# A rotary embedding kernel writes 512 KB of zeros to its output first, from the ScalarE queue

## Chip, cores, metric

One core of a Trainium2 chip. The metric is the time of one execution in device microseconds.

## The reference

```python
batch, seq_len, num_heads, head_dim = 8, 2048, 16, 64     # x: (8, 2048, 16, 64) float32; cos, sin: (2048, 32)
x1, x2 = x[..., :32], x[..., 32:]
out1 = x1 * cos - x2 * sin                                # cos, sin broadcast over batch and heads
out2 = x1 * sin + x2 * cos
out  = concatenate([out1, out2], axis=-1)                 # float32
```

x and the output are 67.1 MB each, 8.4 MB per batch.

## The kernel before

```python
P = 128; J = S // P          # 16 rows of the sequence on each partition
NBUF = 5
const_pool = ...tile_pool(bufs=1)
io_pool  = ...tile_pool(bufs=NBUF)        # five float16 tiles of one batch each
tmp_pool = ...tile_pool(bufs=1)           # one float16 tile v

head = const_pool.tile([P, JA, H, D], f32)                 # JA = 2
nc.sync.dma_start(out=head..., in_=x0[:, 0:JA, :]...)      # 1 MB, the first rows of batch 0
# --- the change goes in here ---
nc.sync.dma_start(out=sin_f, in_=sin...)                   # 256 KB
nc.sync.dma_start(out=cos_f, in_=cos...)                   # 256 KB

def load(b):                                               # float32 in DRAM -> float16 in SBUF
    xt = io_pool.tile([P, J, H, D], f16)
    nc.gpsimd.dma_start(out=xt..., in_=x[b]...)
    return xt

def store(b, xt):                                          # float16 in SBUF -> float32 in DRAM
    nc.gpsimd.dma_start(out=out[b]..., in_=xt)

def rotate(xt):                                            # 26.2 us on VectorE
    v = tmp_pool.tile([P, J, H, D], f16)
    nc.vector.tensor_mul(out=v[:, :, :, 0:Dh], in0=xt[:, :, :, Dh:D], in1=neg_b)
    nc.vector.tensor_mul(out=v[:, :, :, Dh:D], in0=xt[:, :, :, 0:Dh], in1=sin_b)
    nc.vector.tensor_mul(out=xw, in0=xw, in1=cos_b)
    nc.vector.tensor_add(out=xa, in0=xa, in1=v...)

tiles = [load(b) for b in range(NBUF)]
nc.scalar.copy(...)                                        # head rows, sin, -sin, cos to float16
for b in range(B):
    rotate(tiles[b])
    if b < B - 1: store(b, tiles[b])
    if b + NBUF < B: tiles.append(load(b + NBUF))
# ... the last batch is stored in three parts
```

All bulk transfers but the first and the last rows (1 MB each, from SyncE) are issued from GpSimd and so share one queue, in program order. Loads 5, 6 and 7 reuse the tiles of batches 0, 1 and 2 and wait for those stores.

## Time and profile before

| | before |
|---|---|
| time, median of 3 runs | 317.48 us |
| span of the profile | 315.6 us |
| DMA share, 2.5 to 313 us, in three long stretches | 1.00 or more |
| VectorE busy | 209.2 us (66%) |
| VectorE ends its last rotation | 263.7 us |

The page of the kernel before: busy time of the engines, the busy tenths in 40 slices, and the queues.

```profile
DVE 209.2 (66%) x32; ACT 6.8 (2%) x6; POOL 9.4 (3%) x21
DVE  0009599999999999999979999990009994000000
DMA  9899999999999999999999999999999999999998
q0 software_dynamic: 2448, 99.09, 98.0%
q1 hardware_dynamic: 576, 2.62, 2.2%
HBM read 67.63 MB, written 67.11 MB: 427 GB/s over the span
```

Here q0 is the queue of GpSimd and q1 that of SyncE. VectorE has idle slices at the start, before its last rotation and during the last 51 us. The DMA row has none. The windows of the same kernel give the DMA share in the column before the last; it is a little over 1 because the recorded times of neighbouring packets overlap: a row of a store is recorded at 2.45 us, but on an engine the rows follow each other every 2.41 us.

```profile
2.50:100.00 97.50, 72.33 (x12) 3.66 (x4) 2.62 (x5) 1.00 1.02 224
100.00:200.00 100.00, 98.07 (x16) 0.00 (x0) 3.01 (x6) 1.00 1.00 346
200.00:313.00 113.00, 38.75 (x6) 1.90 (x1) 2.27 (x5) 1.00 1.01 395
```

The timeline of the kernel before: start, duration, engine, line, operation, and in brackets the idle time before it and what ended that.

```profile
5.45 1.90 ACT L75 CAST xt<-head 128x2048 f16<-128x2048 f32 x1 [3.43 <-DMA head<-in_x_dram]
23.51 4.43 DVE L67 TENSOR_TENSOR v<-xt,neg_h 128x8192 f16<-128x8192 f16 x1 [23.51 <-DMA xt<-in_x_dram]
35.55 0.62 ACT L81 CAST cos_h<-cos_f 128x512 f16<-128x512 f32 x1 [17.98 <-DMA cos_f<-in_cos_dram]
54.18 0.54 POOL L58 DMA_DIRECT2D out_dram<-xt  x1 [50.14 <-DVE xt L72]
121.83 0.53 POOL L51 DMA_DIRECT2D xt<-in_x_dram  x1 [41.14 <-DMA out_dram<-xt]
237.47 4.42 DVE L67 TENSOR_TENSOR v<-xt,neg_h 128x8192 f16<-128x8192 f16 x1 [24.82 <-DMA xt<-in_x_dram]
```

Read it so: rotation 0 starts when load 0 has landed; cos lands late and holds it up once more. Store 0 is issued at 54 us but has landed only at 121.8 us, when load 5 is let go: it stood behind five loads. Rotation 7 (last line) waits 24.8 us for its load. So VectorE waits for the DMA engines at both ends, and they never wait for VectorE.

### The profile page before, as it was taken

The numbers are of one execution on the slowest core, as the hardware profiler recorded it, in microseconds if no ns is written. First come the engines' busy times: TensorE is split into PE (matmuls) and PEld (weight loads), VectorE is DVE, ScalarE is ACT, GpSimd is POOL, SyncE is SP. The second block draws the span as 40 slices with busy tenths as digits, with TensorE's granted clock in tenths as the row PEclk, the third lists the DMA queues.
The fourth block names the chain that finished last, engine by engine and source line by source line (L and its number), as shares of the span: only waits on it lengthen the run. The fifth ranks groups of instructions, "written<-read, shape, count | busy, mean of one in ns | idle before, by whom it ended". The sixth has DMA issues, their size and how long they took to land.

```text
span 315.6 us, 126 instructions
## 1 busy us (share of the span) xinstructions
DVE 209.2 (66%) x32; ACT 6.8 (2%) x6; POOL 9.4 (3%) x21
## 2 busy tenths in 40 slices
DVE  0009599999999999999979999990009994000000
ACT  4010000000000000000000000000000002000000
POOL 3000000000000000010000000100000001000000
DMA  9899999999999999999999999999999999999998
GB/s 278 184 261 207 200 249 216 199 199 249 216 199 266 399 424 507 399 332 233 233 199 199 390 407 399 399 532 266 199 224 507 399 399 498 432 399 399 432 424 341
DMA packets 3024, 101.71 MB, mean 322 GB/s; under 512 B 336, under 2 KB 336, under 8 KB 592
## 3 DMA queue, kind: packets, MB, share of 16 engines
q0 software_dynamic: 2448, 99.09, 98.0%
q1 hardware_dynamic: 576, 2.62, 2.2%
HBM read 67.63 MB, written 67.11 MB: 427 GB/s over the span
## 4 chain that ended last, share of the span: by engine, by line
issue 25%; DMA 23%; DVE 21%; another core or an unknown queue 13%; POOL 1%; ACT 1%; SPq 0%; POOLq 0%; DVEq 0%; ACTq 0%
DMA xt<-in_x_dram 12%; DMA cos_f<-in_cos_dram 11%; DVE xt L70 8%; DVE xt L72 8%; DVE v L68 3%; DVE v L67 1%; ACT head L105 1%; POOL out_dram L58 1%; POOL xt L51 0%; ACT cos_h L81 0%; SPq L45 0%; SPq L36 0%; POOLq L58 0%; DVEq L67 0%
## 5 line engine op out<-in xcount | busy, mean ns | idle before, releaser
L70 DVE TENSOR_TENSOR xt<-xt,cos_h 128x16384 f16<-128x16384 f16 x8 | 69.5, 8692 | 4.2 <-ACT cos_h L81 3.9
L72 DVE TENSOR_TENSOR xt<-xt,v 128x16384 f16<-128x16384 f16 x8 | 69.5, 8692 | 0.3
L67 DVE TENSOR_TENSOR v<-xt,neg_h 128x8192 f16<-128x8192 f16 x8 | 35.4, 4425 | 50.1 <-DMA xt<-in_x_dram 49.9
L68 DVE TENSOR_TENSOR v<-xt,sin_h 128x8192 f16<-128x8192 f16 x8 | 35.3, 4417 | 0.0
L51 POOL DMA_DIRECT2D xt<-in_x_dram x8 | 4.4, 560 | 117.1 <-DMA out_dram<-xt 116.3
L105 ACT CAST head<-xt 128x2048 f32<-128x2048 f16 x1 | 1.9, 1897 | 227.6 <-DVE xt L72 227.6
L58 POOL DMA_DIRECT2D out_dram<-xt x7 | 3.7, 535 | 87.8 <-DVE xt L72 87.8
L95 POOL DMA_DIRECT2D out_dram<-xt x1 | 0.5, 531 | 50.5 <-DVE xt L72 50.5
L75 ACT CAST xt<-head 128x2048 f16<-128x2048 f32 x1 | 1.9, 1898 | 3.4 <-DMA head<-in_x_dram 3.4
L75 ACT ACT_TABLE_LOAD x1 | 1.3, 1283 | 0.7 <-PEq L127 0.7
L81 ACT CAST cos_h<-cos_f 128x512 f16<-128x512 f32 x1 | 0.6, 617 | 18.0 <-DMA cos_f<-in_cos_dram 18.0
L79 ACT CAST sin_h<-sin_f 128x512 f16<-128x512 f32 x1 | 0.6, 617 | 9.1 <-DMA sin_f<-in_sin_dram 9.1
L80 ACT ACTIVATE neg_h<-sin_f 128x512 f16<-128x512 f32 x1 | 0.6, 624 | 0.0
L97 POOL DMA_DIRECT2D out_dram<-xt x1 | 0.5, 531 | 0.0
L127 POOL MEMSET const-float32-0.0<- 128x1 f32 x1 | 0.1, 98 | 0.2 <-issue 0.2
L127 POOL MEMSET const-bfloat16-1.0<- 128x1 bf16 x1 | 0.1, 101 | 0.0
L127 POOL MEMSET const-float32-1.0<- 128x1 f32 x1 | 0.1, 98 | 0.0
L127 POOL MEMSET const-uint8-127<- 128x1 uint8 x1 | 0.1, 98 | 0.0
## 6 DMA issues: line engine op xcount, KB each, us to landing
xt<-in_x_dram POOLq DMA_DIRECT2D x7, 4096.0 KB, 41.1
out_dram<-xt POOLq DMA_DIRECT2D x1, 4608.0 KB, 42.3
xt<-in_x_dram POOLq DMA_DIRECT2D x1, 3584.0 KB, 22.2
out_dram<-xt POOLq DMA_DIRECT2D x1, 2560.0 KB, 47.9
head<-in_x_dram SPq DMA_DIRECT2D x1, 1024.0 KB, 4.7
out_dram<-head SPq DMA_DIRECT2D x1, 1024.0 KB, 8.4
sin_f<-in_sin_dram SPq DMA_DIRECT2D x1, 256.0 KB, 15.2
cos_f<-in_cos_dram SPq DMA_DIRECT2D x1, 256.0 KB, 33.9
```

The source lines that it names most:

```text
L51: nc.gpsimd.dma_start(out=xt[:, j0:J, :, :].rearrange("p j h d -> p (j h d)"), in_=x[b].rearrange("(p j) h d -> p j (h d)", j=J)[:, j0:J, ...
L58: nc.gpsimd.dma_start(out=out[b].rearrange("(p j) h d -> p (j h d)", j=J), in_=xt)
L67: nc.vector.tensor_mul(out=v[:, :, :, 0:Dh], in0=xt[:, :, :, Dh:D], in1=neg_b)
L68: nc.vector.tensor_mul(out=v[:, :, :, Dh:D], in0=xt[:, :, :, 0:Dh], in1=sin_b)
L70: nc.vector.tensor_mul(out=xw, in0=xw, in1=cos_b)
L72: nc.vector.tensor_add(out=xa, in0=xa, in1=v.rearrange("p j h d -> p (j h d)"))
L75: nc.scalar.copy(out=tiles[0][:, 0:JA, :, :].rearrange("p j h d -> p (j h d)"), in_=head.rearrange("p j h d -> p (j h d)"),)
L79: nc.scalar.copy(out=sin_h, in_=sin_f)
L80: nc.scalar.mul(out=neg_h, in_=sin_f, mul=-1.0)
L81: nc.scalar.copy(out=cos_h, in_=cos_f)
L95: gate = nc.gpsimd.dma_start(out=dst, in_=src)
L105: nc.scalar.copy(out=head.rearrange("p j h d -> p (j h d)"), in_=src)
```

## The change

The intent: 512 KB of zeros go to the first contiguous 512 KB of the output early on, from the ScalarE queue, and are overwritten by the result. The zeros use the buffer of v (same tag, one buffer), as v has less than 1 KB per partition left beside it.

```diff
+    W = 1024
+    zero = tmp_pool.tile([P, W], f32, tag="v")
+    nc.vector.memset(zero, 0.0)
+    nc.scalar.dma_start(
+        out=out[0].rearrange("s h d -> (s h d)")[0 : P * W].rearrange("(p f) -> p f", p=P),
+        in_=zero,
     )
```

The order of the instructions on each engine is otherwise unchanged. Two waits are new: the first multiply of rotation 0 and store 0 both wait for the zeros.

More of the change, by code (lines that the diff above doesn't have):

```diff
@@ L38 @@
         in_=x0[:, 0:JA, :].rearrange("p j f -> p (j f)"),
+    )
+    W = 1024
[4 more added lines that the diff above has]
+        in_=zero,
     )
```

## The prediction

> **What bounds the kernel now.** The 16 DMA engines, from start to end. Read by window, the DMA share is 0.93 or more from 2.5 to 314 us of the 315.6 us span; VectorE is busy 66%, ScalarE 2% (the page). The packet records agree: a row of a full batch takes 2.45 us (stores) or 2.43 us (loads) on an engine, 26.8 GB/s, 428 GB/s for 16; the float32 side of all transfers is 134.7 MB, and 134.7 MB / 428 GB/s = 314 us. Loads and stores simply add up.
>
> By the timeline VectorE ends rotation 7 at 263.7 us, and 51 us of stores follow. The first store is issued at 54 us, but the loads ahead of it on its queue keep the engines busy until about 101 us: 45 us of slack.
>
> **What the change adds.**
> - A memset of 128x1024 float32 on VectorE, about 1 us (estimate from the Trainium skill, "VectorE: DVE Perf Modes", section on zero memsets: one cycle per element), while VectorE idles until 23.5 us. Cost 0.
> - One DMA issue on ScalarE (0.4 us, as on SyncE); ScalarE waits for the head rows until 5.45 us anyway. Cost 0.
> - 512 KB more for the DMA engines: 8 packets of 4 KB on each. Packets of 2 KB took 96 ns and of 8 KB 309 ns, so about 167 ns each (interpolated): **1.34 us per engine**. The engines have no gap, so it is added to the end. Another issuing queue gives no more bandwidth (Trainium skill, "DMA: Bandwidth & Descriptors", section "Issuing engines are not separate DMA queues"); the trace agrees in that the queues' shares add up to 100%.
> - New waits: the first multiply of rotation 0 waits until the zeros have landed (they share the buffer of v), and so does store 0 (same bytes of the output). I expect them to land 5 to 20 us in, so neither wait is the last: the multiply waits for load 0 (23.5 us, now about 25), store 0 for VectorE (54 us).
>
> **What it moves.** A 2 KB packet of the tables gets one turn per 2.1 to 2.4 us packet of the loads. Before, some of them slip in before load 0 starts; the zeros now take that time. So cos lands 4 to 9 us later, the multiplication by cos (36.2 us) starts at 40 to 45 us, and rotations 0 to 4 shift as much. VectorE waits for loads at 158.6 us (1.6 us) and before rotation 7 (24.8 us), where the shift vanishes. Every store has tens of us of work ahead of it in the queue, so the order of transfers stays. On the critical path: only the 1.34 us.
>
> **Predicted time.** 317.48 + 1.34 = 318.8 us; 8 in 10: 317.9 to 320.2. Faster by over 2%: 1%; within 2%: 97%; slower by over 2%: 2%.
>
> **What would show it.** 128 more packets, of 4 KB, near 0.17 us each; written bytes up from 67.11 to 67.63 MB; DMA share still full; each landing of a bulk transfer about 1.3 us later (rotation 7 starts at 238.8 instead of 237.5 us); cos later by more than that.
>
> **What would make it wrong.** If the zeros land late (after 30 us), rotation 0 waits for them; still hidden unless it costs over 40 us. If small packets disturb bulk ones (slower 64 KB packets), the cost is larger. If the engines have idle time at the start that the zeros fill, it is smaller, down to 0.5 us. A fixed cost of a third queue would show outside the DMA-busy stretch.

## The result, and the profile after

318.70 us, median of 4 runs (318.46 to 319.15), against 317.42 us for the kernel before (4 runs). The ratio is 1.0041, 95% interval 1.0026 to 1.0056, which is +1.3 us (0.8 to 1.8). The ratios are not quite the ratios of the medians, nor of the plain means of the listed times (big_zeros below: 1.0309 against 1.0314). A difference in us below is this ratio less 1, times the median of the kernel before in the same rounds.

The page of the changed kernel: engines, slices, queues, and the new memset among the groups.

```profile
DVE 210.1 (66%) x33; ACT 6.8 (2%) x6; POOL 9.4 (3%) x21
DVE  1008899999999999999969999990008994000000
DMA  9999999999999999999999999999999999999998
q10 hardware_dynamic: 144, 0.52, 0.4%
HBM read 67.63 MB, written 67.63 MB: 427 GB/s over the span
L42 DVE MEMSET zero<- 128x1024 f32 x1 | 0.9, 912 | 1.0 <-PEq L134 1.0
```

A third queue has appeared (q10, that of ScalarE) with 0.52 MB, the written bytes are up by the same, and the rate over the span is still 427 GB/s. The windows of the changed kernel over the same stretches are again full:

```profile
2.50:100.00 97.50, 73.09 (x12) 4.82 (x5) 2.62 (x5) 1.00 1.04 229
100.00:200.00 100.00, 95.96 (x16) 0.00 (x0) 2.12 (x4) 1.00 1.00 346
200.00:313.00 113.00, 40.10 (x6) 1.90 (x1) 3.16 (x6) 1.00 1.00 390
```

The timeline of the changed kernel, the same instructions as before with the issue of the zeros in front (lines of the file moved by 7):

```profile
1.97 0.37 ACTq L43 DMA_DIRECT2D out_dram<-zero  x1
5.53 1.90 ACT L82 CAST xt<-head 128x2048 f16<-128x2048 f32 x1 [1.88 <-DMA head<-in_x_dram]
25.22 4.42 DVE L74 TENSOR_TENSOR v<-xt,neg_h 128x8192 f16<-128x8192 f16 x1 [23.29 <-DMA out_dram<-zero]
34.79 0.62 ACT L88 CAST cos_h<-cos_f 128x512 f16<-128x512 f32 x1 [18.48 <-DMA cos_f<-in_cos_dram]
53.42 0.54 POOL L65 DMA_DIRECT2D out_dram<-xt  x1 [49.38 <-DVE xt L79]
123.18 0.54 POOL L58 DMA_DIRECT2D xt<-in_x_dram  x1 [43.24 <-DMA out_dram<-xt]
238.82 4.42 DVE L74 TENSOR_TENSOR v<-xt,neg_h 128x8192 f16<-128x8192 f16 x1 [24.82 <-DMA xt<-in_x_dram]
```

Load 5 is let go 1.35 us later (123.18 against 121.83) and rotation 7 starts 1.35 us later (238.82 against 237.47). VectorE, on the other hand, is *early* in between: store 0 was ready 0.8 us sooner than before, and yet it landed later. That alone says that the transfers ahead of store 0, not VectorE, set the time.

Two things are not as predicted: rotation 0 was released by the zeros, and cos came earlier, not later. The DMA issues of the changed kernel (size and time from issue to landing):

```profile
xt<-in_x_dram POOLq DMA_DIRECT2D x1, 3584.0 KB, 23.5
out_dram<-zero ACTq DMA_DIRECT2D x1, 512.0 KB, 23.1
cos_f<-in_cos_dram SPq DMA_DIRECT2D x1, 256.0 KB, 33.1
```

The first of these, load 0, was issued at 1.25 us and so landed at 24.75 us; the zeros were issued at 1.97 us and landed at 25.07 us, 0.3 us behind. The packet records show why they took 23 us. Starts are counted from the first DMA packet of the execution; each figure in brackets is the number of packets in a group, over 16 engines.

```
load 0's first packet                3.4 us (each then takes 2.13 us on its engine)
zeros, 4 KB packets of 0.160 us      5.7 (16), 8.0 (16), 10.3 (16), 12.7 (16), 15.0 (16), 17.4 (16), 19.8 (16), 22.1 (16)
sin and cos, 2 KB packets            2.9 (101), then 10 to 16 per turn, 30 at 22.0, last at 30.0
```

The records do not name the engine, but groups of 16, one turn apart, say that each engine serves its queues in turn: one row of load 0 (2.13 us), one packet of zeros, one of the tables. The zeros came too late to run before load 0 began and so needed eight full turns. The same records show the cost directly: the rows of load 0 follow each other every 2.19 us in the kernel before and every 2.35 us in the changed one, 0.16 us for each of the eight packets of zeros, together 1.3 us.

### The profile page after: what moved, and what is told of

Its sections match the earlier page's. It is cut to its first block, busy times and chain, and to the rows that moved or that the text cites. A ratio compares the mean times of both kernels' runs of the same rounds, so it can differ in the third digit from the quotient of the medians.

```text
span 317.0 us, 131 instructions
## 1 busy us (share of the span) xinstructions
DVE 210.1 (66%) x33; ACT 6.8 (2%) x6; POOL 9.4 (3%) x21
## 4 chain that ended last, share of the span: by engine, by line
issue 25%; DMA 23%; DVE 21%; another core or an unknown queue 14%; POOL 1%; ACT 1%; SPq 0%; POOLq 0%; DVEq 0%; ACTq 0%
DMA xt<-in_x_dram 12%; DMA cos_f<-in_cos_dram 10%; DVE xt L77 8%; DVE xt L79 8%; DVE v L75 3%; DVE v L74 1%; ACT head L112 1%; POOL out_dram L65 0%; POOL xt L58 0%; ACT cos_h L88 0%; SPq L52 0%; SPq L36 0%; POOLq L65 0%; DVEq L74 0%
## 5 line engine op out<-in xcount | busy, mean ns | idle before, releaser
L75 DVE TENSOR_TENSOR v<-xt,sin_h 128x8192 f16<-128x8192 f16 x8 | 35.3, 4418 | 0.0
L42 DVE MEMSET zero<- 128x1024 f32 x1 | 0.9, 912 | 1.0 <-PEq L134 1.0
## 6 DMA issues: line engine op xcount, KB each, us to landing
xt<-in_x_dram POOLq DMA_DIRECT2D x1, 3584.0 KB, 23.5
```

The source lines that it names most:

```text
L42: nc.vector.memset(zero, 0.0)
```

## The experiments

Main theory ("bytes"): the engines are full from 2.5 us to the last 2 us, so the cost is the engine time of the added packets, 128 packets x 160.4 ns / 16 engines = 1.28 us, wherever they run. Rivals: the later start of rotation 0 (25.2 instead of 23.5 us), the VectorE work, or a fixed cost of a DMA on a third queue. Twelve runs were made, all with a correct result: nine other kernels, the changed kernel once more, and the kernel before twice.

| run | difference, us (95%) | first multiply, us | rotation 7, us |
|---|---|---|---|
| after_again | +1.2 (0.8 to 1.6) | 25.7 | 238.6 |
| memset_only | 0.0 (-0.3 to 0.4) | 24.4 | 238.2 |
| zeros_on_sync | +1.0 (0.6 to 1.3) | 51.8 | 238.8 |
| other_buffer | +1.4 (1.0 to 1.7) | 25.1 | 238.6 |
| tiny_zeros | -0.3 (-0.7 to 0.0) | 24.0 | 237.1 |
| big_zeros | +9.8 (9.4 to 10.3) | 47.6 | 248.0 |
| cos_on_scalar | -0.2 (-0.5 to 0.2) | 27.6 | 237.5 |
| copy_in_dram | +1.5 (1.0 to 2.0) | 25.3 | 238.5 |
| tiny_late | -0.1 (-0.5 to 0.3) | 24.6 | 237.7 |
| behind_loads | +36.1 (35.5 to 36.6) | 103.5 | 287.3 |

### after_again: the changed kernel once more

> The changed kernel again, to pin its cost within a tighter interval and to see what of its trace repeats. Every theory: the kernel before plus 1.3 us (1.1 to 1.5). Turn theory (one packet of the zeros per bulk packet of load 0 on each engine): the zeros land about 25 us into the span again, in 8 groups of 16 packets. Landing of cos: I could not predict it; if it differs by up to one bulk packet (2.4 us) from the 34.8 us of the first profile, the earlier landing there was chance and not an effect of the change.

Edit: none. 318.84 us, ratio 1.0037 (1.0025 to 1.0049). The zeros ran in the same eight groups of 16, from 5.7 to 22.2 us, and released rotation 0 again. The copy of cos started at 32.2 us, 2.55 us earlier than in the first profile of the same kernel (a little more than the 2.4 us written down): that landing moves by about one turn from run to run.

### memset_only: without the DMA

```diff
-    nc.scalar.dma_start(
-        out=out[0].rearrange("s h d -> (s h d)")[0 : P * W].rearrange("(p f) -> p f", p=P),
-        in_=zero,
-    )
```

> The memset without its DMA. Byte theory (the engines are full, 128 packets of 160 ns cost 1.28 us per engine): 0 us beside the kernel before (within 0.2). Rival that says the VectorE work or the new tile in the buffer of v costs: up to +1.3 us. The first multiply starts at about 23.5 us, released by load 0.

317.75 us, ratio 1.0001 (0.9989 to 1.0013). The memset and its tile show no cost (within -0.3 to 0.4 us). The first multiply started at 24.4 us, not 23.5: it was released by load 0, whose landing thus varies by 0.9 us without zeros in flight. The profiled execution was the slowest of the five (318.14 us, rotation 7 at 238.2 us), so a single profile is good to some 0.7 us only; the cost is read from the timed runs.

### zeros_on_sync: rotation 0 twice as late

```diff
     nc.sync.dma_start(out=cos_f, in_=cos...)
+    nc.sync.dma_start(out=out[0]...[0 : P * W]..., in_=zero)      # and no DMA on nc.scalar
```

> The zeros go out on the SyncE queue behind sin and cos, instead of on the ScalarE queue. On that queue 24 small packets per engine then take turns one after the other, so the zeros should land at about 50 us (45 to 55) and rotation 0 starts then instead of at 25 us. Byte theory: still +1.3 us (1.1 to 1.5), as 25 us more of delay for VectorE at the start fit into the slack; rotation 7 still starts at about 238.8 us. Rival that says the 1.3 us come from the later start of rotation 0 (25.2 instead of 23.5 us): about +25 us. Rival that says a third queue costs: +0.

318.65 us, ratio 1.0030 (1.0018 to 1.0042). The point is a little under the expected 1.1 to 1.5 us, the interval reaches into it. Its timeline:

```profile
51.82 4.43 DVE L74 TENSOR_TENSOR v<-xt,neg_h 128x8192 f16<-128x8192 f16 x1 [49.89 <-DMA out_dram<-zero]
238.82 4.43 DVE L74 TENSOR_TENSOR v<-xt,neg_h 128x8192 f16<-128x8192 f16 x1 [3.24 <-DMA xt<-in_x_dram]
```

Rotation 0 started 26.6 us later than in the changed kernel, and rotation 7 at the same 238.82 us: the idle time before it shrank from 24.8 to 3.2 us. The rival of the later rotation 0 asks for about +25 us and is out; so is the third queue, as there were only two here.

### other_buffer: the multiply does not wait for the zeros

```diff
-    zero = tmp_pool.tile([P, W], f32, tag="v")
+    zero = io_pool.tile([P, W], f32, tag="xt")
```

> The zeros lie in a buffer of the big tiles and not in that of v (v has no room beside it), so the first multiply does not wait for them; load 4 waits for them instead, behind four queued loads. Byte theory: +1.3 us as for the changed kernel, and rotation 0 starts when load 0 has landed, about 24.9 us instead of 25.2. Rival that says the wait on the zeros costs: less than +1.3, down to 0.

319.02 us, ratio 1.0043 (1.0031 to 1.0055). The first multiply was released by load 0 as expected; load 4 waited for the zeros instead, and was issued at 25.65 us:

```profile
25.05 4.42 DVE L74 TENSOR_TENSOR v<-xt,neg_h 128x8192 f16<-128x8192 f16 x1 [23.11 <-DMA xt<-in_x_dram]
25.65 0.53 POOL L58 DMA_DIRECT2D xt<-in_x_dram  x1 [22.14 <-DMA out_dram<-zero]
```

Without the wait of VectorE on the zeros the cost is the same, within the intervals.

### tiny_zeros: 8 KB instead of 512 KB

```diff
-    W = 1024
+    W = 16
```

> 8 KB of zeros instead of 512 KB: the same memset, DMA, third queue, waits and number of packets (8 per engine), but 64 bytes in each. Byte theory: +0.1 us (0 to 0.3). Rival that says a DMA on a third queue has a fixed cost: +1.3 us. Turn theory: the zeros still land about 23.5 us in, as each of the 8 packets still waits for one packet of load 0.

317.23 us, ratio 0.9989 (0.9977 to 1.0001): no fixed cost of 1.3 us of a DMA on a third queue, of its issue or of its waits. The landing was missed: the packets ran in one burst 2.1 us after the first DMA packet, before load 0, and landed at 5.7 us. The memset of 16 columns took 0.07 us, so this DMA was issued at 0.92 and not at 1.97 us. And then the effect came that I had predicted for the change itself: only 81 packets of the tables got in before load 0 (99 in the profile before the change), and cos came late, in this one profile: at 38.4 us, against 33.4 to 35.8 us in the five profiles with cos in its old place and nothing written early (before, before_b, before_c, memset_only, behind_loads). Its timeline, and the line of its DMA issues:

```profile
0.92 0.37 ACTq L43 DMA_DIRECT2D out_dram<-zero  x1
38.43 0.62 ACT L88 CAST cos_h<-cos_f 128x512 f16<-128x512 f32 x1 [18.30 <-DMA cos_f<-in_cos_dram]
```
```profile
out_dram<-zero ACTq DMA_DIRECT2D x1, 8.0 KB, 4.8
```

### big_zeros: 4 MB

```diff
-    W = 1024
+    W = 8192
```

> 4 MB of zeros, 8 times as many bytes in the same number of packets (32 KB each, about 1.22 us by the 26.8 GB/s of the bulk packets). Byte theory: +9.8 us (9.2 to 10.4). Rivals of a fixed cost: +1.3 us. Turn theory: the zeros land just after load 0, which itself lands about 9.8 us later than before, so rotation 0 starts at 33 to 35 us and this too is hidden.

327.83 us, ratio 1.0309 (1.0295 to 1.0324), +9.8 us as expected. Eight times the bytes cost 7.5 times the 1.30 us of the change. The 128 packets of 32 KB took 1.217 us each, 9.74 us per engine. The start of rotation 0 was missed (47.6 us instead of 33 to 35): the memset took 6.88 us, and ScalarE issued this DMA only at 14.5 us, behind its copy of sin, since the order on ScalarE had changed. This was hidden as well.

### cos_on_scalar: the kernel before, cos on the ScalarE queue

```diff
-    nc.sync.dma_start(out=cos_f, in_=cos...)
+    nc.scalar.dma_start(out=cos_f, in_=cos...)
```

> The kernel before, without zeros, but cos is loaded from the ScalarE queue. Byte theory: the same time (within 0.2 us), as no byte is added. Turn theory: sin and cos now take turns side by side and not one after the other, so cos lands at 20 to 26 us instead of 35.5 us and the multiplication by cos no longer waits for it. It also shows when a DMA issued on ScalarE at the start gets its first packet: if the small packets of the ScalarE queue run among those of the head rows (before about 5 us), the late start of the zeros (about 7.4 us) was due to their being issued 1.2 us later; if they too start only with or after load 0, the ScalarE queue itself starts late.

317.42 us, ratio 0.9995 (0.9983 to 1.0006), as expected. The landing of cos was missed: all its 128 packets ran in one burst 0.7 us after the first DMA packet, and the copy of cos started at 8.7 us. Sin then got its first packet only 8.0 us after the first DMA packet, behind the second row of load 0, and one more per turn, so that rotation 0 waited for sin until 27.6 us. So the ScalarE queue is not late in itself; what is issued on it at 0.74 us runs before load 0. The time did not care.

### copy_in_dram: 512 KB of x instead of zeros, memory to memory

```diff
-    zero = tmp_pool.tile([P, W], f32, tag="v")
-    nc.vector.memset(zero, 0.0)
     nc.scalar.dma_start(
         out=out[0]...[0 : P * W]...,
-        in_=zero,
+        in_=x[0].rearrange("s h d -> (s h d)")[0 : P * W].rearrange("(p f) -> p f", p=P),
     )
```

> Instead of zeros, the first 512 KB of x are copied to the same place in the output, memory to memory, with no memset and no buffer of v; built as 16 pieces of 32 KB, so one packet per engine. Byte theory: +1.22 us by the rate of the bulk packets (1.1 to 1.5). Rivals that need the memset or the wait on v: 0. Turn theory: it lands after at most two bulk packets, by 10 us, and rotation 0 starts at about 24.8 us, released by load 0.

318.88 us, ratio 1.0047 (1.0032 to 1.0063). One packet of 32 KB per engine, 1.213 us each, landed at 9.1 us. The cost is there with neither memset nor buffer of v. This run also tells engine time from memory traffic, a rival that the list above leaves out: the copy reads 0.52 MB and writes 0.52 MB, as its page shows:

```profile
HBM read 68.16 MB, written 67.63 MB: 429 GB/s over the span
```

If the bytes at the memory set the cost, these 1.05 MB would take 2.5 us at the 427 GB/s of the page before, which lies outside the interval of 1.0 to 2.0 us; the engine time, 1.21 us, lies inside. Here no packet of the tables got in before load 0: sin came so late that it released rotation 0 (25.3 us, and not load 0 at 24.8 us, as was expected; the multiply by sin runs first here), and cos was copied at 44.7 us, 9 us late. Both were hidden.

### tiny_late: 8 KB again, but issued late

```diff
-        out=out[0]...[0 : P * W]...,
-        in_=zero,
+        out=out[0]...[0 : P * 16]...,
+        in_=zero[:, 0:16],
```

> The memset as in the changed kernel (128x1024), but only 16 columns of it (8 KB) are written out. In the run with 8 KB and a short memset the small packets ran before load 0; in the changed kernel they waited for its packets. If the late issue (2.0 instead of 0.9 us) is the reason, the 8 KB now take one turn per packet of load 0 in 8 groups of 16, start about 5.7 us after the first DMA packet and land 23 to 25 us in; if the size of the packets is the reason, they run in one burst before load 0 again. Time: the same as before (within 0.3 us) either way.

317.45 us, ratio 0.9997 (0.9984 to 1.0009). The 64-byte packets ran in eight groups of 16 from 5.6 to 21.0 us and landed at 24.5 us. So the issue at 1.97 us, behind the memset, was why the zeros took eight turns, and not their size. Its timeline, and the line of its DMA issues, to be held against those of tiny_zeros:

```profile
1.97 0.37 ACTq L43 DMA_DIRECT2D out_dram<-zero  x1
24.61 4.42 DVE L74 TENSOR_TENSOR v<-xt,neg_h 128x8192 f16<-128x8192 f16 x1 [22.68 <-DMA out_dram<-zero]
```
```profile
out_dram<-zero ACTq DMA_DIRECT2D x1, 8.0 KB, 22.5
```

### behind_loads: the zeros beyond the slack

```diff
     tiles = [load(b) for b in range(NBUF)]
+    nc.gpsimd.dma_start(out=out[0]...[0 : P * W]..., in_=zero)    # and no DMA on nc.scalar
```

> The same 512 KB of zeros are issued on the GpSimd queue behind the five loads, so they land only at about 103 us, and rotation 0, which waits for them, starts then, 78 us late instead of 1.7. This is beyond the 45 us of slack: store 0 is ready at about 130 us and the engines idle from about 103 to 130 us and again for some us before store 1. Adding up the queue by 19.4 us per batch from there gives about 353 us, +35 us (27 to 43). The byte theory without the slack (only bytes count, whatever the waits) says +1.3 us.

353.83 us, ratio 1.1136 (1.1119 to 1.1153). Its windows, with the DMA share before the last column:

```profile
100.00:104.00 4.00, 0.53 (x1) 0.00 (x0) 0.00 (x0) 1.00 0.33 131
104.00:130.00 26.00, 25.83 (x5) 0.00 (x0) 0.00 (x0) 1.00 0.00 0
130.00:150.00 20.00, 19.93 (x4) 0.00 (x0) 0.54 (x1) 1.00 0.98 419
150.00:156.00 6.00, 6.00 (x1) 0.00 (x0) 0.00 (x0) 1.00 0.01 0
156.00:351.00 195.00, 156.87 (x24) 1.90 (x1) 5.84 (x11) 1.00 1.01 366
```

The engines idle for 26 us, 6 us and two thirds of 4 us, together 34.7 us; with the 1.3 us of the zeros this is 36.0 of the 36.1 us. The same bytes cost 1.3 us or 36 us, depending on whether the wait that hangs on them outlasts the work queued on the engines.

### before_b and before_c: two more profiles of the unchanged kernel

> The unchanged kernel, for one more profile. In three profiles without early zeros the copy of cos started at 35.5 to 35.8 us; in five with zeros (or 8 KB of them) issued at 2 us it started at 31.0 to 34.8 us. If this is chance (how many table packets each engine gets in before load 0), this profile lies anywhere between 31 and 36 us. If the zeros really bring cos forward, it lies at 35.3 to 36 us again.

> The same once more, for the same question: chance says anywhere between 31 and 36 us in at least one of the two; a real effect of the zeros says 35.3 to 36 us in both.

The copy of cos, first in before_b, then in before_c:

```profile
35.57 0.62 ACT L81 CAST cos_h<-cos_f 128x512 f16<-128x512 f32 x1 [17.97 <-DMA cos_f<-in_cos_dram]
```
```profile
33.44 0.62 ACT L81 CAST cos_h<-cos_f 128x512 f16<-128x512 f32 x1 [17.74 <-DMA cos_f<-in_cos_dram]
```

The second answer lies outside 35.3 to 36 us, so it is chance: the unchanged kernel has both 35.6 and 33.4 us, one turn apart, as the changed one has 34.8 and 32.2. A small tendency of the zeros to bring cos forward is not excluded by so few profiles; it touches no time.

## Why the prediction was right

The time was right (318.8 predicted, 318.7 measured), by the mechanism predicted.

- **The engines have no gap, so added packets are added time.** Right. Share still full, rotation 7 at 238.82 us as predicted (238.8; in the table, 512 KB of added bytes give 238.5 to 238.8 us, none or 8 KB 237.1 to 238.2 us), cost in proportion to bytes: about 0 for 8 KB, 1.3 us for 512 KB, 9.8 us for 4 MB. The last is 4.19 MB / 9.8 us = 428 GB/s (408 to 448 by its interval), the rate that the prediction read from the packets of the kernel before.
- **The size.** 8 packets of 167 ns, interpolated, were 8 packets of 160 ns: 1.28 instead of 1.34 us.
- **The queue does not matter, the engines are shared** (Trainium skill, "DMA: Bandwidth & Descriptors", section "Issuing engines are not separate DMA queues"). This agrees: ScalarE's queue +1.2 and +1.3, SyncE's +1.0 us, intervals overlapping; and cos moved to the other queue, -0.2 us with 0 inside its interval.
- **No cost from the memset, the issue, the waits.** Right, as far as the intervals reach (some 0.4 us): memset_only 0.0, tiny_late -0.1 us.
- **"I expect them to land 5 to 20 us in, so neither wait is the last."** Wrong: they landed at 25.1 us, and rotation 0 waited for them, 0.3 us longer than for load 0. The failed step is the start of the zeros. I had them share the time before load 0; they were issued 2 us in, behind the memset, came up on the engines after load 0's first row, and then took one turn of 2.3 us per packet. tiny_zeros (issued at 0.92 us) and tiny_late (1.97 us) tell that apart.
- **"The zeros now take that time. So cos lands 4 to 9 us later."** Wrong for the change, by the same step: cos came 0.8 us earlier in the profile shown, within the spread that the unchanged kernel has of its own. The mechanism exists where the small DMA does come in time: cos 2.9 us late in tiny_zeros and 9.1 us late in copy_in_dram, against 35.55 us.
- **The slack.** Right: 45 us were estimated between VectorE and the queue; a delay of 28 us (zeros_on_sync) cost nothing beyond the bytes, one of 80 us (behind_loads) cost 35 us of idle engines. The 80 us less these 35 leave 45 us, as estimated; no run with a delay between 28 and 80 us tried where it ends.

What stays open: what the time between the issue of the zeros (1.97 us) and their first packet consists of, that is why they were not on the engines before load 0 began. Their first packet started 5.4 us after the issue, of which one row of load 0 can be 2.1 us; in tiny_zeros it was 2.9 us and for cos in cos_on_scalar 1.7 us.

## What to carry to other kernels

Where the DMA engines are full from end to end, price a transfer by its engine time (packets per engine times the length of one), whichever queue issues it and whatever VectorE does meanwhile. Then check the waits that come with it: a scratch buffer shared with a transfer makes compute wait for that transfer, which is free only as long as the queued work outlasts the wait. In these runs a small transfer beside bulk ones landed not after its bytes but after its number of packets per engine times the length of a bulk packet (8 turns of 2.2 to 2.4 us, for 8 KB and for 512 KB alike), so try to issue it before the bulk begins.

## What the Trainium skill lacked or had wrong

- "VectorE: DVE Perf Modes", section "Zero memsets can be issued as uint32 (trn2)": a memset takes one cycle per element, at a clock that the page gives as 0.96 GHz, hence my estimate of about 1 us for 1024 elements. Measured: 0.912 us for 1024 and 6.88 us for 8192 float32 elements per partition, so (6.88 - 0.912) us / 7168 = 0.83 ns per element, faster than the 1.04 ns of the page.
- "DMA: Bandwidth & Descriptors", section "SWDGE vs HWDGE vs iDMA", has packets preferably of at most 4096 B as the unit between which an engine switches its queues, and has the engine take them in turn. Here a queue beside GpSimd's got one turn per whole row of a load: 56 KB read, 2.13 us, for 2 KB, 4 KB and 64-byte packets alike. The page does not say that such a packet can be a whole row of a load, so that small transfers started beside it need packets x row time: 8 KB took 22.5 us to land, and 4.8 us when issued 1 us earlier.
- No page that I read lists the engine time of single packets of 2 to 32 KB; here 2 KB took 91, 4 KB 160 (171 in zeros_on_sync), 8 KB about 309 and 32 KB 1217 ns (1213 in copy_in_dram).
